# Channel-mixer weights split by two DMAs and ACT instead of a load, ACT and DVE

## The chip, the cores and the metric

The kernel runs on one core of a Trainium2 chip. Five engines work side by side, each through its own queue in order: PE (TensorE, matrix products), DVE (VectorE), ACT (ScalarE), POOL (GpSimd) and SP (SyncE, which here only issues transfers); 16 DMA engines move data between the chip's memory (HBM) and the on-chip memory (SBUF). The metric is the device time of one execution in microseconds. The trace of one execution is read beside the times.

## The reference, cut to what matters

One encoder layer on 512 tokens of width 1024, all in float32. An attention part (two token mixers, gates, output projection) gives `x`; then comes the channel mixer, which the change touches, and a last norm:

```python
h = rms_norm(x, norm_ffn[l])
x = x + (jax.nn.silu(h @ w_gate_ffn[l]) * (h @ w_up_ffn[l])) @ w_down_ffn[l]
return rms_norm(x, norm_final)
```

`w_gate_ffn` and `w_up_ffn` are 1024 x 2816, `w_down_ffn` is 2816 x 1024.

## The kernel before

PE multiplies fast in float32r, a rounded form of float32. To keep float32's accuracy every operand is split in two float32r tiles: `hi`, the rounded value, and `lo`, what rounding left (value minus `hi`). `mm3` (L87) then adds three products, hi x hi, hi x lo and lo x hi; lo x lo is left out.

Weights come in units of 128 x 1024 float32 (512 KB). `load_unit` (L77) does four things for one unit: SP issues a load into a raw tile (three buffers, tag `raw`), ACT rounds it into `whi` (`split_hi`, L68), and DVE subtracts `whi` from the raw tile into `wlo` (`split_lo`, L75). `whi` and `wlo` have five buffers each, used in turn by all units of the program. A buffer is free again when PE has done the unit's last product.

The channel mixer works with 66 units. The 2816 hidden features are 22 blocks of 128 (`f` = 0 to 21). For each, `gu(f)` loads a gate unit (`fg`) and an up unit (`fu`); `ffn_in` (L596) runs 8 x 3 products for each over the 512 tokens, applies a sigmoid on ACT and two multiplications on DVE, and splits the result into `ah` and `al`. The first two blocks are done in two token halves of 256. From `f` = 3 on, after every second block, `down0(u)` adds one unit of the output weights (`d0`, two hidden blocks by 512 output columns) for the four token tiles. After block 21 the second 512 output columns follow, with 11 more units (`d1`); the last two of them are loaded together and used token tile by token tile, so that each tile's last norm and output can start early. In the middle of the stage units are thus used in groups of five: gate, up, gate, up, down.

Ahead of the channel mixer stands the output projection (`w_out`, units `o0` and `o1`). Its second half holds four units until its last token tile is done; each token tile's norm (`norm_tile`, L531) uses ACT, DVE and a power on POOL (L108), and PE transposes the result.

The order on each engine is not written out: a scheduler of the framework sorts the instructions by a model of their times when the program is built, and sets the signals between the engines. Each engine then works through its list in order, and an instruction that waits for a signal holds up all behind it on its engine.

Of the kernel before, what the change touches and what calls it, by code (L numbers as in the profile page):

```python
# [9 lines left out]
F32 = mybir.dt.float32  # L10
F32R = mybir.dt.float32r
AF = mybir.ActivationFunctionType
ALU = mybir.AluOpType
# [6 lines left out]
P = 128  # L20
# [7 lines left out]
UNIT = 1024  # L28
# [6 lines left out]
def kernel(  # L35
# [19 lines left out]
    v, a, g, pe = nc.vector, nc.scalar, nc.gpsimd, nc.tensor  # L55

    def pool(stack, name, bufs=1, space=None, side=None):
        kw = {} if space is None else {"space": space}
        if side is not None:
            kw["side"] = side  # L60
        return stack.enter_context(tc.tile_pool(name=name, bufs=bufs, **kw))
# [3 lines left out]
    wp = pool(ctx, "wp", bufs=5)  # L65

    def split_hi(dst, src):
        a.copy(dst, src)  # L68
# [5 lines left out]
    def split_lo(dst, src, hi):  # L74
        v.tensor_tensor(out=dst, in0=src, in1=hi.bitcast(F32), op=ALU.subtract)  # L75

    def load_unit(src, nm, n=UNIT, raw_tile=None):  # L77
        raw = wp.tile([P, UNIT], F32, tag="raw", bufs=3, name=f"raw_{nm}") if raw_tile is None else raw_tile
        raw = raw[:, :n]
        nc.sync.dma_start(raw, src)  # L80
        hi = wp.tile([P, UNIT], F32R, tag="whi", name=f"whi_{nm}")[:, :n]
        lo = wp.tile([P, UNIT], F32R, tag="wlo", name=f"wlo_{nm}")[:, :n]
        split_hi(hi, raw)
        split_lo(lo, raw, hi)
        return hi, lo

    def mm3(acc, lh, ll, rh, rl, start, stop):  # L87
# [48 lines left out]
    for u in range(4):  # L136
        xr = up.tile([P, UNIT], F32, tag="u", name=f"xr{u}")
        if u < 2:
            rkv = up.tile([P, UNIT], F32, tag="u", name=f"rkv{u}")
        if u == 0:  # L140
            khi = wp.tile([P, UNIT], F32R, tag="whi", name="whi_akv0")
            klo = wp.tile([P, UNIT], F32R, tag="wlo", name="wlo_akv0")
            units_kv.append((khi, klo))
            for j in range(2):
                c = slice(j * S, (j + 1) * S)
                nc.sync.dma_start(xr[:, c], xT[0][:, c])
                nc.scalar.dma_start(rkv[:, c], w_in[4][:, c])
            for j in range(2):
                c = slice(j * S, (j + 1) * S)
                split_scaled(xgh[:, j, :], xgl[:, j, :], xr[:, c], gmix[:, j:j + 1])  # L150
                split_hi(khi[:, c], rkv[:, c])
                split_lo(klo[:, c], rkv[:, c], khi[:, c])
        else:
            nc.sync.dma_start(xr, xT[u])
            if u == 1:
                units_kv.append(load_unit(w_in[5], "akv1", raw_tile=rkv))
            for j in range(2):
                kt = 2 * u + j
                split_scaled(xgh[:, kt, :], xgl[:, kt, :], xr[:, j * S:(j + 1) * S], gmix[:, kt:kt + 1])
        xrs.append(xr)  # L160
    units_q = [load_unit(w_in[u], f"aq{u}", raw_tile=up.tile([P, UNIT], F32, tag="u", name=f"raq{u}")) for u in range(4)]
    for u in range(4):
        sq = up.tile([P, 2, S], F32, tag="u", name=f"sqx{u}")
# [156 lines left out]
    def group_b(h, parts):  # L320
        us = [load_unit(w_in[6 + 4 * h + u, :, :768], f"b{h}_{u}", 768) for u in range(4)]
        vt = u_tile(f"vb{h}", shape=(P, NT, 2, P))
        qT = u_tile(f"qTb{h}")
        kT = [u_tile(f"kTb{h}_{i}") for i in range(2)]
        for tt in range(NT):
            nm = f"b{h}_{tt}"
            t = slice(tt * P, (tt + 1) * P)
            acc = ps_mm.tile([P, S], F32, tag="mm", name=f"acc_{nm}")[:, :384]
            for kt in range(KT):
                hi, lo = us[kt // 2]  # L330
                o = (kt % 2) * 384
                mm3(acc, xgh[:, kt, t], xgl[:, kt, t], hi[:, o:o + 384], lo[:, o:o + 384], kt == 0, kt == KT - 1)
            z = tmp.tile([P, S], F32, tag="q", name=f"z_{nm}")
            a.activation(z[:, :128], acc[:, :128], AF.Copy, scale=rstd8[:, tt:tt + 1])
            a.activation(z[:, 128:384], acc[:, 128:384], AF.Copy, scale=rstd[:, tt:tt + 1])
            split_hi(vt[:, tt, 0, :], z[:, 256:384])
            split_lo(vt[:, tt, 1, :], z[:, 256:384], vt[:, tt, 0, :])
            qs = pack_heads(do_rope(z[:, :256].rearrange("p (n h d) -> p n h d", n=1, d=HD), tabs["b"], tt, nm), 4, 2, nm)
            transpose_heads([qs[:, 0, 0:P], qs[:, 1, 0:P]] + pair(qs, 2), [qT, kT[0]], tt, f"{nm}_0")
            transpose_heads(pair(qs, 3), [kT[1]], tt, f"{nm}_1")  # L340
            if tt == NT - 1:
                parts[:] = [qT, kT, vt]
            yield True
# [144 lines left out]
    for qd in range(4):  # L488
# [7 lines left out]
        for br in range(2):  # L496
            oh, ol = osplit[br]
            for j in range(2):
                ct = 2 * qd + j
                hi, lo = us[j]  # L500
# [110 lines left out]
    def down(acc, u, wu, tt, c0=0, c1=S):  # L611
        hi, lo = wu
        t = slice(tt * P, (tt + 1) * P)
        for j in range(2):
            f = 2 * u + j
            w = slice(j * S + c0, j * S + c1)
            mm3(acc, ah[:, f, t], al[:, f, t], hi[:, w], lo[:, w], f == 0, f == NF - 1)

    def gu(f):
        return load_unit(w_gu[2 * f], f"fg{f}"), load_unit(w_gu[2 * f + 1], f"fu{f}")  # L620

    acc0 = None

    def down0(u):
        wu = load_unit(w_down[u], f"d0_{u}")
        for tt in range(NT):
            down(acc0[tt], u, wu, tt)

    gu01 = [gu(0), gu(1)]
    for t0 in (0, 256):  # L630
        for f in range(2):
            ffn_in(f, t0, t0 + 256, *gu01[f])
    for f in range(1, NF):
        if f > 1:
            ffn_in(f, 0, S, *gu(f))
        if f == 1:
            acc0 = [ps_d.tile([P, S], F32, tag="pd", name=f"pd0_{tt}") for tt in range(NT)]
        if f >= 3 and f % 2 == 1:
            u = (f - 3) // 2
            down0(u)  # L640
    down0(10)

    s3 = const.tile([P, 3, NT], F32, name="s3")
# [18 lines left out]
                 (ps_g.tile([P, S], F32, tag="pg", name="pd1_4")[:, :H], H, S)])  # L662
    NLAST = 2
    for u in range(11 - NLAST):
        wu = load_unit(w_down[11 + u], f"d1_{u}")
        for tt in range(NT):
            for acc, c0, c1 in acc1[tt]:
                down(acc, u, wu, tt, c0, c1)
    last = [load_unit(w_down[11 + u], f"d1_{u}") for u in range(11 - NLAST, 11)]
    for tt in range(NT):  # L670
        for i, (acc, c0, c1) in enumerate(acc1[tt]):
            for u in range(NLAST):
# [96 lines left out]
```

## Time and profile before

| | us |
|---|---|
| median of 3 runs | 769.11 |
| lowest, highest | 768.08, 769.47 |
| the profiled execution | 766.71 |
| its span in the trace | 764.7 |
| PE, DVE, ACT, POOL busy in the span | 745.6, 412.5, 337.2, 102.7 |

Times in the trace are microseconds from the start of the span. A row of an instruction names its line in the kernel, its engine, what it writes and reads; names lose their numbers, so `wlo_fg` stands for all gate units. PE's matmuls overlap: the trace gives one some 0.39 us, but the next starts 0.23 us later, so PE's pace is read from starts. "Busy" of PE counts any time in which a matmul is under way. PEclk is the clock that PE was granted, as a share of 2.4 GHz. In the table of DMA issues the last number is the median time from issue to landing.

### The profile page before, as it was taken

How to read it: one execution, taken by the hardware profiler on the slowest of the kernel's cores; microseconds unless marked ns; L12 is line 12 of the kernel's file. 1: busy time of each engine (PE TensorE's matmuls, PEld its weight loads, DVE VectorE, ACT ScalarE, POOL GpSimd, SP SyncE). 2: the span in 40 equal slices, each digit the busy share in tenths (PEclk: the TensorE clock that was granted, in tenths of full speed). 3: DMA queues.
4: the chain of work that ended last, by engine and by line, in shares of the span. 5: the costliest groups of instructions: out<-in, count | busy, mean ns of one | idle time of the engine just before them, and what ended most of it. 6: DMA issues, size and time to landing. Idle time of an engine off the chain costs nothing.

```text
span 764.7 us, 9837 instructions
## 1 busy us (share of the span) xinstructions
PE 745.6 (97%) x3786; PEld 638.5 (83%) x3786; DVE 412.5 (54%) x668; ACT 337.2 (44%) x606; POOL 102.7 (13%) x126
## 2 busy tenths in 40 slices
PE   5999999999999999999999999999999999999996
PEld 4889887799988888888889888888888888888885
DVE  5778698669795564494375433332423333335114
ACT  6457698777667665232153222222222322233203
POOL 3656342223221010100000000000000000000001
PEclk9999999999999999999999999999999999999998
DMA  8122021002141212344223332323232333232202
GB/s 331 64 84 83 29 68 58 21 22 85 29 136 60 78 56 83 137 138 138 82 83 111 111 109 84 110 86 108 86 107 91 102 94 100 90 103 84 82 1 111
DMA packets 21071, 69.52 MB, mean 91 GB/s; under 512 B 2592, under 2 KB 2848, under 8 KB 21024
## 3 DMA queue, kind: packets, MB, share of 16 engines
q1 hardware_dynamic: 18432, 63.45, 25.1%
q10 hardware_dynamic: 2592, 5.45, 2.0%
q8 instruction: 30, 0.49, 0.3%
q14 instruction: 17, 0.14, 0.1%
HBM read 66.79 MB, written 2.10 MB: 90 GB/s over the span
## 4 chain that ended last, share of the span: by engine, by line
PE 94%; DVE 2%; DMA 2%; ACT 1%; issue 1%; POOL 0%; POOLq 0%; ACTq 0%; SPq 0%; DVEq 0%
PE pg L89 5%; PE pu L89 5%; PE pu L90 5%; PE pg L90 5%; PE pg L88 5%; PE pu L88 5%; PE pd L89 5%; PE pd L88 5%; PE pd L90 5%; PE gt L89 4%; PE gt L88 4%; PE gt L90 4%; PE acc_b L89 3%; PE acc_b L88 3%; PE acc_b L90 3%; PE pp L88 2%
## 5 line engine op out<-in xcount | busy, mean ns | idle before, releaser
L89 PE MATMUL pd<-wlo_d,ah 128*128 128x512 f32 (+1 forms) x198 | 72.5, 366 | 0.0
L88 PE MATMUL pd<-whi_d,ah 128*128 128x512 f32 (+1 forms) x198 | 72.4, 366 | 0.0
L90 PE MATMUL pd<-whi_d,al 128*128 128x512 f32 (+1 forms) x198 | 72.0, 365 | 0.0
L88 PE MATMUL pg<-hh,whi_fg 128*128 128x512 f32 (+1 forms) x192 | 71.4, 372 | 0.0
L90 PE MATMUL pu<-hh,wlo_fu 128*128 128x512 f32 (+1 forms) x192 | 71.4, 372 | 0.0
L89 PE MATMUL pg<-hl,whi_fg 128*128 128x512 f32 (+1 forms) x192 | 71.3, 371 | 0.0
L88 PE MATMUL pu<-hh,whi_fu 128*128 128x512 f32 (+1 forms) x192 | 71.3, 371 | 0.0
L89 PE MATMUL pu<-hl,whi_fu 128*128 128x512 f32 (+1 forms) x192 | 71.3, 371 | 0.0
L90 PE MATMUL pg<-hh,wlo_fg 128*128 128x512 f32 (+1 forms) x192 | 71.3, 371 | 0.0
L75 DVE TENSOR_TENSOR wlo_d<-raw_d,whi_d 128x1024 fp32r<-128x1024 f32 x22 | 26.9, 1225 | 72.4 <-ACT whi_d L68 72.4
L75 DVE TENSOR_TENSOR wlo_fg<-raw_fg,whi_fg 128x1024 fp32r<-128x1024 f32 x22 | 27.0, 1225 | 70.0 <-ACT whi_fg L68 69.9
L68 ACT CAST whi_d<-raw_d 128x1024 fp32r<-128x1024 f32 x22 | 23.2, 1053 | 85.4 <-issue 42.3
L68 ACT CAST whi_fg<-raw_fg 128x1024 fp32r<-128x1024 f32 x22 | 23.2, 1053 | 78.8 <-PE pg L89 41.2
L68 ACT CAST whi_fu<-raw_fu 128x1024 fp32r<-128x1024 f32 x22 | 23.2, 1053 | 72.7 <-PE pu L89 69.1
L88 PE MATMUL gt<-xgh,whi_g 128*128 128x512 f32 x128 | 50.6, 395 | 0.0
L90 PE MATMUL gt<-xgh,wlo_g 128*128 128x512 f32 x128 | 50.5, 395 | 0.0
L89 PE MATMUL gt<-xgl,whi_g 128*128 128x512 f32 x128 | 50.5, 394 | 0.0
L683 POOL TENSOR_TENSOR r<-mf,mhalf 128x1 f32<-128x1 f32 x4 | 2.3, 586 | 356.9 <-DVE mf L681 356.9
L607 DVE TENSOR_TENSOR sg<-pu,sg 128x512 f32<-128x512 f32 (+1 forms) x24 | 15.4, 646 | 54.8 <-PE pu L90 54.8
L89 PE MATMUL acc_b<-wlo_b,xgh 128*128 128x384 f32 x128 | 43.6, 341 | 0.0
L90 PE MATMUL acc_b<-whi_b,xgl 128*128 128x384 f32 x128 | 43.4, 339 | 0.0
L88 PE MATMUL acc_b<-whi_b,xgh 128*128 128x384 f32 x128 | 43.3, 339 | 0.0
(278 smaller groups left out, 1832.9 us busy)
## 6 DMA issues: line engine op xcount, KB each, us to landing
raw_fg<-in_w_gu_dram SPq DMA_DIRECT2D x22, 512.0 KB, 3.3
raw_fu<-in_w_gu_dram SPq DMA_DIRECT2D x22, 512.0 KB, 3.3
raw_d<-in_w_down_dram SPq DMA_DIRECT2D x22, 512.0 KB, 3.3
raw_g<-in_w_in_dram SPq DMA_DIRECT2D x16, 512.0 KB, 3.3
raw_b<-in_w_in_dram SPq DMA_DIRECT2D x16, 384.0 KB, 3.6
raw_p<-in_w_proj_dram SPq DMA_DIRECT2D x8, 512.0 KB, 3.3
raw_o<-in_w_out_dram SPq DMA_DIRECT2D x8, 512.0 KB, 3.3
raq<-in_w_in_dram SPq DMA_DIRECT2D x4, 512.0 KB, 7.3
```

The source lines that it names most:

```text
L68: a.copy(dst, src)
L75: v.tensor_tensor(out=dst, in0=src, in1=hi.bitcast(F32), op=ALU.subtract)
L88: pe.matmul(acc, lhsT=lh, rhs=rh, start=start, stop=False)
L89: pe.matmul(acc, lhsT=lh, rhs=rl, start=False, stop=False)
L90: pe.matmul(acc, lhsT=ll, rhs=rh, start=False, stop=stop)
L607: v.tensor_tensor(out=t_, in0=pu, in1=t_, op=ALU.mult)
L683: g.tensor_tensor(out=r3, in0=ms, in1=mhalf[:, 0:1], op=ALU.pow)
```

## The change

The channel mixer's 66 units no longer go through `load_unit` but through a new function, `load_unit_dma`. POOL issues a DMA that reads the float32 weights from HBM and writes them rounded, as float32r, into `whi`. ACT writes the negative of `whi` into `wlo`. POOL issues a second DMA that reads the same weights again and adds them to `wlo` where they land, so that `wlo` holds weight minus `whi`. Raw tiles and the subtraction on DVE are not used for these units. All other units stay with `load_unit`. The new function stands ahead of `mm3`, so later lines move down by eight in the changed kernel's own rows.

```diff
@@ -82,6 +82,14 @@
         lo = wp.tile([P, UNIT], F32R, tag="wlo", name=f"wlo_{nm}")[:, :n]
         split_hi(hi, raw)
         split_lo(lo, raw, hi)
+        return hi, lo
+
+    def load_unit_dma(src, nm):
+        hi = wp.tile([P, UNIT], F32R, tag="whi", name=f"whi_{nm}")
+        lo = wp.tile([P, UNIT], F32R, tag="wlo", name=f"wlo_{nm}")
+        g.dma_start(hi, src)
+        a.activation(lo, hi.bitcast(F32), AF.Copy, scale=-1.0)
+        g.dma_start(lo, src, accum_op=ALU.add)
         return hi, lo
...
     def gu(f):
-        return load_unit(w_gu[2 * f], f"fg{f}"), load_unit(w_gu[2 * f + 1], f"fu{f}")
+        return load_unit_dma(w_gu[2 * f], f"fg{f}"), load_unit_dma(w_gu[2 * f + 1], f"fu{f}")
...
     def down0(u):
-        wu = load_unit(w_down[u], f"d0_{u}")
+        wu = load_unit_dma(w_down[u], f"d0_{u}")
...
     for u in range(11 - NLAST):
-        wu = load_unit(w_down[11 + u], f"d1_{u}")
+        wu = load_unit_dma(w_down[11 + u], f"d1_{u}")
...
-    last = [load_unit(w_down[11 + u], f"d1_{u}") for u in range(11 - NLAST, 11)]
+    last = [load_unit_dma(w_down[11 + u], f"d1_{u}") for u in range(11 - NLAST, 11)]
```

The scheduler's lists change with it. In the middle of the channel mixer, SP's list before held the loads of one group of five units and the next, one row a unit (the name's first number is the block, the last is the tile's own):

```order
L80 DMA raw_fg8_5001<-in_w_gu_dram 128x1024
L80 DMA raw_fu8_5007<-in_w_gu_dram 128x1024
L80 DMA raw_fg9_5069<-in_w_gu_dram 128x1024
L80 DMA raw_fu9_5075<-in_w_gu_dram 128x1024
L80 DMA raw_d0_3_5137<-in_w_down_dram 128x1024
L80 DMA raw_fg10_5167<-in_w_gu_dram 128x1024
L80 DMA raw_fu10_5173<-in_w_gu_dram 128x1024
```

The same units now stand in POOL's list, two rows a unit (L90 the rounding DMA, L92 the adding one):

```order
L90 DMA whi_fg8_4982<-in_w_gu_dram 128x1024
L90 DMA whi_fu8_4987<-in_w_gu_dram 128x1024
L92 DMA wlo_fg8_4983<-in_w_gu_dram 128x1024
L92 DMA wlo_fu8_4988<-in_w_gu_dram 128x1024
L90 DMA whi_fg9_5048<-in_w_gu_dram 128x1024
L92 DMA wlo_fg9_5049<-in_w_gu_dram 128x1024
L90 DMA whi_fu9_5053<-in_w_gu_dram 128x1024
L90 DMA whi_d0_3_5114<-in_w_down_dram 128x1024
L92 DMA wlo_fu9_5054<-in_w_gu_dram 128x1024
L92 DMA wlo_d0_3_5115<-in_w_down_dram 128x1024
L90 DMA whi_fg10_5143<-in_w_gu_dram 128x1024
L90 DMA whi_fu10_5148<-in_w_gu_dram 128x1024
```

Between the rounding row and the adding row of a unit stands at most one other unit's rounding row, and the next pair begins behind the adding rows of the last.

At the start of the channel mixer POOL's list before held only the powers of the norm tiles (`r2`) and, after the whole stage, of the last norm (`r3`):

```order
L108 TENSOR_TENSOR rsb_3_3393<-ms_3394,mhalf_73 128x4
L108 TENSOR_TENSOR r2_0_4094<-ms_4095,mhalf_73 128x1
L108 TENSOR_TENSOR r2_1_4142<-ms_4143,mhalf_73 128x1
L108 TENSOR_TENSOR r2_2_4190<-ms_4191,mhalf_73 128x1
L108 TENSOR_TENSOR r2_3_4213<-ms_4214,mhalf_73 128x1
L683 TENSOR_TENSOR r3_0_6577<-mf_0_6573,mhalf_73 128x1
```

Now the DMAs of the first five units stand among them:

```order
L90 DMA whi_fu0_4256<-in_w_gu_dram 128x1024
L116 TENSOR_TENSOR r2_2_4190<-ms_4191,mhalf_73 128x1
L90 DMA whi_fg1_4261<-in_w_gu_dram 128x1024
L90 DMA whi_fu1_4266<-in_w_gu_dram 128x1024
L90 DMA whi_fg2_4499<-in_w_gu_dram 128x1024
L92 DMA wlo_fu0_4257<-in_w_gu_dram 128x1024
L116 TENSOR_TENSOR r2_3_4213<-ms_4214,mhalf_73 128x1
L92 DMA wlo_fg1_4262<-in_w_gu_dram 128x1024
L92 DMA wlo_fu1_4267<-in_w_gu_dram 128x1024
L92 DMA wlo_fg2_4500<-in_w_gu_dram 128x1024
```

The power of the third norm tile stands behind one rounding DMA, that of the fourth behind four of them and the first of their adding DMAs.

## Rows read from the trace of the kernel before

**Rows 1.** Head of the page: span; busy time of each engine.
```profile
span 764.7 us, 9837 instructions
...
PE 745.6 (97%) x3786; PEld 638.5 (83%) x3786; DVE 412.5 (54%) x668; ACT 337.2 (44%) x606; POOL 102.7 (13%) x126
```

**Rows 2.** Table by stretches, two stretches of the channel mixer.
```profile
core 0: us, PE busy (x) PEld busy (x) DVE busy (x) ACT busy (x) POOL busy (x), PEclk, DMA share, GB/s
...
585.00:640.00 55.00, 55.00 (x245) 45.53 (x244) 20.42 (x23) 14.59 (x18) 0.00 (x0) 1.00 0.30 96
...
695.00:750.00 55.00, 55.00 (x294) 47.58 (x293) 13.22 (x19) 9.95 (x15) 0.00 (x0) 1.00 0.14 48
```

**Rows 3.** Timeline of PE, end of the output projection (start, duration).
```profile
389.75 0.48 PE L88 MATMUL po<-whi_o,yh 128*128 128x512 f32 x1
...
393.93 0.39 PE L88 MATMUL po<-whi_o,yh 128*128 128x512 f32 x1
...
395.29 0.28 PE L88 MATMUL pg<-hh,whi_fg 128*128 128x256 f32 x1
395.40 0.28 PE L89 MATMUL pg<-hl,whi_fg 128*128 128x256 f32 x1
```

**Rows 4.** Timeline of SP's queue, one group of five loads.
```profile
460.46 0.33 SPq L80 DMA_DIRECT2D raw_d<-in_w_down_dram  x1
465.94 0.33 SPq L80 DMA_DIRECT2D raw_fg<-in_w_gu_dram  x1
...
487.66 0.33 SPq L80 DMA_DIRECT2D raw_d<-in_w_down_dram  x1
```

**Rows 5.** Groups of instructions (count, busy us, mean ns, idle before, releaser).
```profile
L75 DVE TENSOR_TENSOR wlo_fg<-raw_fg,whi_fg 128x1024 fp32r<-128x1024 f32 x22 | 27.0, 1225 | 70.0 <-ACT whi_fg L68 69.9
...
L68 ACT CAST whi_fg<-raw_fg 128x1024 fp32r<-128x1024 f32 x22 | 23.2, 1053 | 78.8 <-PE pg L89 41.2 <-issue 31.6 <-PE po L90 4.4
...
L377 POOL TENSOR_SCALAR p_a<-p_a,r_a 128x512 f32<-128x512 f32 x32 | 22.7, 711 | 53.1 <-DVE r_a L355 48.0 <-PE sc_a L348 1.9 <-PE ptp_a L361 1.2
```

**Rows 6.** Timelines of ACT and DVE, start and middle of the channel mixer.
```profile
394.17 1.06 ACT L68 CAST whi_fu<-raw_fu 128x1024 fp32r<-128x1024 f32 x1 [0.31 <-PE po L90]
...
395.81 1.22 DVE L75 TENSOR_TENSOR wlo_fu<-raw_fu,whi_fu 128x1024 fp32r<-128x1024 f32 x1
...
562.48 0.59 ACT L605 ACTIVATE sg<-pg 128x512 f32<-128x512 f32 x1
...
567.88 0.61 ACT L68 CAST ah<-sg 128x512 fp32r<-128x512 f32 x1
```

**Rows 7.** Table by stretches, start of the program.
```profile
14.00:16.00 2.00, 1.33 (x11) 1.12 (x10) 1.62 (x3) 2.00 (x4) 1.92 (x2) 1.00 1.03 400
16.00:20.00 4.00, 0.43 (x4) 0.23 (x2) 4.00 (x2) 0.31 (x1) 3.74 (x2) 0.99 1.03 413
20.00:30.00 10.00, 9.58 (x59) 9.05 (x59) 9.89 (x13) 6.50 (x11) 7.06 (x6) 0.83 0.12 47
```

**Rows 8.** DMA issues (count, KB each, us from issue to landing).
```profile
raw_fg<-in_w_gu_dram SPq DMA_DIRECT2D x22, 512.0 KB, 3.3
...
raq<-in_w_in_dram SPq DMA_DIRECT2D x4, 512.0 KB, 7.3
...
out_dram<-xg SPq DMA_DIRECT2D x4, 256.0 KB, 2.0
```

**Rows 9.** Timeline of POOL, first and last power of the last norm.
```profile
752.03 0.54 POOL L683 TENSOR_TENSOR r<-mf,mhalf 128x1 f32<-128x1 f32 x1 [350.70 <-DVE mf L681]
...
759.99 0.55 POOL L683 TENSOR_TENSOR r<-mf,mhalf 128x1 f32<-128x1 f32 x1 [1.52 <-DVE mf L681]
```

**Rows 10.** Table by stretches, end of the program.
```profile
758.60:760.00 1.40, 0.00 (x0) 0.00 (x0) 1.29 (x5) 1.04 (x3) 0.01 (x1) 1.00 0.00 0
760.00:762.00 2.00, 0.00 (x0) 0.00 (x0) 0.49 (x1) 0.72 (x1) 0.53 (x1) 0.65 0.73 278
762.00:764.70 2.70, 0.00 (x0) 0.00 (x0) 0.00 (x0) 0.00 (x0) 0.00 (x0) 0.50 0.48 186
```

## The prediction

> **What bounds the kernel now.** I read the page's busy line first: PE is busy 745.6 of 764.7 us, DVE 412.5, ACT 337.2 [rows 1]. That is an average over stages, so the table by stretches came next. In the channel mixer, from 420 to 750 us, PE is busy for the whole of each of six stretches of 55 us (two stand in the group) at a granted clock of 1.00, that is 2.4 GHz; DVE, which the change relieves, is busy about 20 of 55 us in five of them [rows 2]. The matmul rows give PE's step: six 512-column matmuls start between 393.93 and 395.29, 0.2267 us each [rows 3]. A unit of weights feeds 24 of them (8 of 512 columns, three products each; for the output weights 2 x 4 x 3), so PE eats a unit in 24 x 0.2267 = 5.44 us, and the group of five that recurs (gate, up, gate, up, down) in 27.2 us. SyncE's load rows agree: from one raw_d to the next 487.66 - 460.46 = 27.20 us [rows 4]. So nothing taken off DVE can shorten this stage; the question is whether units still arrive every 5.44 us.
>
> **What is removed.** 66 subtractions on DVE, of which I take one of 1.225 us as the measure [rows 5]: 66 x 1.225 = 81 us of DVE. Their cover is PE's 5.44 us per unit, so they are worth 0. The 66 loads on SyncE go; they were issued when a subtraction freed a raw tile, three units ahead of need, and nothing waited for them. ACT loses 66 rounding copies of 1.053 us [rows 5] and gains 66 negations. No negation is in the trace; the nearest rows on ACT are these copies and the sigmoid of 512 columns at 0.59 beside a copy of 512 at 0.61 [rows 6], so I take 1.05, which changes nothing for ACT.
>
> **What is added.** 132 DMAs on POOL, until now idle in this stage, two for each unit, with a round trip between them: the rounded part must land, ACT must negate it, and only then may the adding DMA be issued. POOL's queue is worked in order, and the order listed in the section on the change settles the matter: the next unit's rounded load mostly stands behind the previous unit's adding DMA. With such a queue the five buffers no longer overlap the units freely. A group of five units holds three serial round trips: (fg8, fu8 together), (fg9), (fu9, d0_3 together).
>
> The parts of a round trip, bounded from rows:
> - h, the transfer of a rounded load. In the stage the DMA engines are busy 0.30 of the time with one load per 5.44 us: 1.63 us [rows 2]. In the crowded stretch from 14 to 16 us they moved 400 GB/s, which makes 524,288 bytes 1.31 us [rows 7]. I take 1.6. Whether rounding slows the transfer no row shows; the upper bound is twice, 3.2.
> - a, the transfer of an adding DMA. It reads the weights again, reads its destination in SBUF, and writes. Lower bound 1.3 as above, if the second read is free; upper bound 4.8, if two reads and a write each cost a whole transfer. The nearest row for an SBUF read by DMA is the output store, 256 KB in 2.0 us from issue to landing, beside 3.3 for a load of 512 KB [rows 8]: a read of SBUF costs about what a load of as many bytes does. So I take load plus read, 2 x 1.6 = 3.2.
> - r, the rest of a landing: 3.3 from issue to landing [rows 8], less SyncE's issue of 0.33 [rows 4], less 1.3: 1.7.
> - n, the negation and its signals: 1.05 + 0.05.
> - p, POOL's issue of one DMA. The lower bound is SyncE's 0.33 [rows 4]. POOL's own work takes 0.54 for one element per partition [rows 9] and 0.71 for 512 [rows 5]; two such pieces of work (a list of reads, one of writes) would be 1.4, the upper bound. I take 1.0.
>
> That one queue's transfers follow each other is seen at the start of the program, where four loads issued together land 7.3 us after issue, not 3.3 [rows 8]. So a round trip is p + (its adding transfers) + h + r + n: the hi transfer waits behind the adding ones issued before it. In a group the three trips carry all five adding transfers: 5a + 3(p + h + r + n) = 5a + 3 x 5.4 = 5a + 16.2. With a = 3.2 that is 32.2 us against PE's 27.2: 5.0 us late per group. The engines' own work is 5 x (1.6 + 3.2) = 24 us, under 27.2: what binds is the order in POOL's queue, not DMA capacity. It decides from a = (27.2 - 16.2)/5 = 2.2 on.
>
> In the second half of the down projection POOL does two trips for three units: 3 x 3.2 + 2 x 5.4 = 20.4 against 16.3, 4.1 late per three.
>
> At the start of the stage the mixer's first units used to lie in raw tiles, with 1.05 + 1.22 us on ACT and DVE to go [rows 6]. Now their loads wait until the output projection's last pass frees buffers: its last token tile begins at 389.75, and the first buffer is free six matmuls later, at about 391.3 [rows 3]. POOL issues four rounded loads before the first of their adding DMAs (the fourth waits for the pass's end, 395.3), so wlo_fu0 is issued at about 396.4 and lands p + a + r = 5.9 later, 402.3. PE has its 24 half matmuls of fg0 from 395.29 (2.9 us, 0.12 each [rows 3]), then parts that need only rounded weights and the last transposes: about 4 us are lost. POOL's power for the last norm tile stands behind wlo_fu0's DMA and moves by about as much, inside this loss.
>
> **The sum.** Some 44 units in 8.8 groups run at the late pace: 8.8 x 5.0 = 44. Twelve units of the output weights at the end, 4 x 4.1 = 16. Start 4. Less what is loaded ahead when the late pace begins, two units, 2 x 5.44 = 11. Together +53. The profiled execution took 766.71 us, so 820; the median of the runs shown, 769.11, lies 2.4 above it, so I say 822. Before any loss the end of the program is unchanged: POOL's last powers come after all its DMAs, as before [rows 9].
>
> Two prices stand only in the Trainium skill. Its page "Collectives: The Full Stack", section "The bandwidth ceiling: the fold count and why AG ≠ RS ≠ AR", says that an addition inside a DMA costs no cycles of its own but needs two reads, which halves the rate: by that a is twice a load, 3.2 with my 1.6 and 2.6 with 1.3, and the sum +53 or about +18. No run here shows it yet. The page "DMA: Bandwidth & Descriptors", section "Specifications", gives a first byte of about 1 us to DMAs issued from GpSimd and 0.6 to those from SyncE: 0.4 more per trip, +1.2 a group, and the sum +67.
>
> **Rivals.**
> - Hidden, not slower (or hardly). The place is the same queue, the price a. If an adding DMA is no dearer than a load, 1.3 to 1.6, a group takes 22.7 to 24.2 us, PE never waits in steady state, and the last twelve units need 15.6 per three, under 16.3. Only the start is left, 0 to 2 us: 767 to 771. For it: the read of SBUF may overlap the other read. Against it: every path of more than 2.2. Chance 0.22, half of it within the bound of 0.2% (1.5 us), which is about what a measurement of this kernel can tell from no change.
> - Dearer yet. If a = 4.8, a group is 40.2: 8.8 x 13.0 + 4 x 8.9 + 7 - 11 = +146, 915; if rounding doubles h as well as a = 3.2, three trips take 4.8 more: 53 + 42 + 13 = +108, 877. Chance 0.25.
> - The clock. PE idle from about 15 to 20 us was followed by a stretch at 0.83, and after its last matmul the granted clock fell from 1.00 to 0.5 (1.2 GHz) at about 760.6 [rows 7, 10]. With idle pieces of 1 to 4 us in each group PE might run partly at the lower level. A stretch of 10 us at 0.83 loses 1.7 us; three per group lose 5.1, about the slack of 5.0 that PE then has, so this is covered unless the clock stays down: PE at 1.2 GHz needs 54.4 a group, and the stage's 360 us would double, some 1,120. Chance 0.03 for most of that.
> - It doesn't do what it says: POOL's issue could be so cheap and landings so early that the start gains too, since the DVE is free for the first tiles. That is worth at most 1 to 3 us, 764 to 768. Chance 0.04.
>
> The forecast itself (a between 2.2 and 4, +10 to +100): 0.46. So faster by over 0.2% 0.05, within 0.2% 0.10, slower 0.85. The range runs from 769, the hidden case, to 930, the dear one with the later first byte; about 0.2 is outside, more of it above.
>
> **What would show it.** Right: PE idle in each group of the channel mixer, ended by the landing of wlo tiles or by ACT; one down unit to the next about 32 us apart where it was 27.2; ACT's negations waiting for the landing of whi tiles; POOL's DMAs waiting for ACT, seldom for PE; DVE some 81 us lighter. The hidden rival: PE full from 420 to 750 as now. The steps can be checked singly: the landing of the adding DMA against that of the rounded load, POOL's issue against 1.0, and the DMA engines' share, which should rise from 0.30 to about 24/32 = 0.75. I would be wrong in kind if PE waits for its weights although POOL's queue stands empty, or if the loss sits at the start alone.

## The result, and the profile after

The changed kernel takes 814.86 us (median of four runs, 814.28 to 816.40), the kernel before 768.60 (four runs, 767.55 to 769.47): ratio 1.0606, 95% interval 1.0593 to 1.0620. It is slower by 46 us; 822 was forecast. The profiled execution took 814.78 us, its span is 812.6.

From the page of the changed kernel: span, busy time of each engine, DMA queue of POOL (packets, MB, share of 16 engines), the chain that ended last, and the landings of a `fu` unit's two DMAs.

```profile
span 812.6 us, 9858 instructions
...
PE 763.2 (94%) x3786; PEld 647.0 (80%) x3786; DVE 338.1 (42%) x602; ACT 336.2 (41%) x606; POOL 196.2 (24%) x258
...
q0 software_dynamic: 19008, 69.21, 36.6%
...
PE 46%; issue 35%; POOL 10%; DMA 5%; DVE 2%; ACT 2%; POOLq 0%; SPq 0%; ACTq 0%; DVEq 0%
...
whi_fu<-in_w_gu_dram POOLq DMA_DIRECT2D x22, 512.0 KB, 6.6
wlo_fu<-in_w_gu_dram POOLq DMA_DIRECT2D x22, 512.0 KB, 5.6
```

DVE's busy time fell by 74 us [rows 1] and ACT kept its 336, yet the span grew by 47.9. The chain that ended last is PE for only 46% of the span; the rest runs through POOL, the transfers and "issue", time in which the engine waited for nothing that the profile shows. The table by stretches shows where PE stopped being full; the first of these rows answers to [rows 2].

```profile
585.00:640.00 55.00, 50.59 (x213) 40.76 (x213) 7.61 (x11) 13.33 (x17) 12.20 (x17) 0.97 0.73 173
640.00:695.00 55.00, 52.32 (x230) 42.55 (x229) 8.30 (x12) 13.83 (x18) 14.16 (x20) 1.00 0.75 175
```

PE is busy 50.6 of 55 us where it was 55.0, and does 213 matmuls (rows that the trace holds) where it did 245. The DMA share (second number from the right) rose from 0.30 to 0.73.

Four starts of PE's matmuls cut the stage into three parts: the first gate product, the first and the last down product, and the last up product between them. Timeline of PE before (the first gate product, 395.29, stands in [rows 3]):

```profile
441.83 0.39 PE L88 MATMUL pd<-whi_d,ah 128*128 128x512 f32 x1
...
686.40 0.39 PE L90 MATMUL pu<-hh,wlo_fu 128*128 128x512 f32 x1
...
758.30 0.28 PE L90 MATMUL pd<-whi_d,al 128*128 128x256 f32 x1
```

And after:

```profile
395.92 0.28 PE L96 MATMUL pg<-hh,whi_fg 128*128 128x256 f32 x1
...
448.97 0.39 PE L96 MATMUL pd<-whi_d,ah 128*128 128x512 f32 x1
...
720.17 0.39 PE L98 MATMUL pu<-hh,wlo_fu 128*128 128x512 f32 x1
...
805.96 0.28 PE L98 MATMUL pd<-whi_d,al 128*128 128x256 f32 x1
```

Start of the stage: 46.54 us before, 53.05 after, +6.5. Groups of five: 244.57 and 271.20, +26.6. Output weights at the end: 71.90 and 85.79, +13.9. Together +47.0; of the rest, 0.6 was there before the stage began and 0.2 lies behind its last product. The same cut is made for every kernel below, each time in its profiled execution, which lies up to 3.4 us off the median of that kernel's runs.

POOL's timeline, three round trips, shows what sets the pace (L90 issues a rounding DMA, L92 an adding one; in brackets the idle time before, and what ended it):

```profile
509.59 0.87 POOL L92 DMA_DIRECT2D wlo_fg<-in_w_gu_dram  x1 [7.26 <-ACT wlo_fg L91]
511.06 0.85 POOL L92 DMA_DIRECT2D wlo_fu<-in_w_gu_dram  x1 [0.60 <-ACT wlo_fu L91]
511.61 0.86 POOL L90 DMA_DIRECT2D whi_fg<-in_w_gu_dram  x1
520.21 0.85 POOL L92 DMA_DIRECT2D wlo_fg<-in_w_gu_dram  x1 [7.74 <-ACT wlo_fg L91]
520.75 0.88 POOL L90 DMA_DIRECT2D whi_fu<-in_w_gu_dram  x1
521.29 0.89 POOL L90 DMA_DIRECT2D whi_d<-in_w_down_dram  x1
528.42 0.87 POOL L92 DMA_DIRECT2D wlo_fu<-in_w_gu_dram  x1 [6.24 <-ACT wlo_fu L91]
529.64 0.86 POOL L92 DMA_DIRECT2D wlo_d<-in_w_down_dram  x1 [0.35 <-ACT wlo_d L91]
530.19 0.87 POOL L90 DMA_DIRECT2D whi_fg<-in_w_gu_dram  x1
530.73 0.88 POOL L90 DMA_DIRECT2D whi_fu<-in_w_gu_dram  x1
539.06 0.88 POOL L92 DMA_DIRECT2D wlo_fg<-in_w_gu_dram  x1 [7.45 <-ACT wlo_fg L91]
```

POOL issues a rounding DMA and stands for 6 to 8 us until ACT has negated what it brought. A trip with two adding DMAs takes 10.62 us (509.59 to 520.21, 528.42 to 539.06), one with a single adding DMA 8.21. The three make 29.5 us for five units (29.4 in the two groups that follow); PE needs 27.2 [rows 4]. The table of waits of the stage from 420 us on names the links (waits, times, longest):

```profile
ACT wlo_fg L91 <- DMA whi_fg<-in_w_gu_dram: 135.9, 19, 9.6
POOL wlo_fg L92 <- ACT wlo_fg L91: 134.2, 19, 9.7
...
POOL whi_fg L90 <- PE pu L98: 2.3, 1, 2.3
```

ACT waits for the landing, POOL for ACT, and POOL for PE once, 2.3 us: buffers are not what is short. In the DMA engines' busy tenths, 505 to 532 us in 40 slices of 0.675 us, the trips are seen as gaps:

```profile
DMA  9999980003999999999600003988999993000969
```

In each trip the engines work for about 7 us and then stand for 2 to 3, while the last transfer's landing is signalled, ACT negates and POOL issues.

At the start of the stage, the table by stretches; then the issue of a DMA by POOL and the row of PE that waits for it:

```profile
402.00:404.00 2.00, 0.00 (x0) 0.00 (x0) 0.72 (x2) 1.78 (x3) 0.88 (x2) 0.85 0.99 195
404.00:406.00 2.00, 0.37 (x1) 0.38 (x2) 1.40 (x3) 0.52 (x2) 0.41 (x1) 0.50 1.10 219
406.00:408.00 2.00, 2.00 (x11) 2.00 (x11) 0.00 (x0) 0.00 (x0) 0.00 (x0) 0.50 1.04 262
408.00:410.00 2.00, 2.00 (x11) 2.00 (x11) 0.00 (x0) 0.00 (x0) 0.00 (x0) 0.50 1.03 270
410.00:412.00 2.00, 2.00 (x18) 2.00 (x17) 0.85 (x2) 0.41 (x1) 0.00 (x0) 0.94 1.11 225
```

```profile
397.49 0.89 POOL L92 DMA_DIRECT2D wlo_fu<-in_w_gu_dram  x1 [0.59 <-ACT wlo_fu L91]
...
405.63 0.58 PE L98 MATMUL pu<-hh,wlo_fu 128*128 128x256 f32 x1 [3.98 <-DMA wlo_fu<-in_w_gu_dram]
```

PE stood 3.98 us for the adding DMA of wlo_fu0, and the granted clock (third number from the right) fell from 1.00 to 0.50, that is from 2.4 to 1.2 GHz, and stayed there until about 410.

### The profile page after: what moved, and what is told of

Its sections match the earlier page's. It is cut to its first block, busy times and chain, and to the rows that moved or that the text cites. A ratio compares the mean times of both kernels' runs of the same rounds, so it can differ in the third digit from the quotient of the medians.

```text
span 812.6 us, 9858 instructions
## 1 busy us (share of the span) xinstructions
PE 763.2 (94%) x3786; PEld 647.0 (80%) x3786; DVE 338.1 (42%) x602; ACT 336.2 (41%) x606; POOL 196.2 (24%) x258
## 3 DMA queue, kind: packets, MB, share of 16 engines
q1 hardware_dynamic: 8928, 28.84, 10.5%
## 4 chain that ended last, share of the span: by engine, by line
PE 46%; issue 35%; POOL 10%; DMA 5%; DVE 2%; ACT 2%; POOLq 0%; SPq 0%; ACTq 0%; DVEq 0%
PE gt L97 4%; PE gt L96 4%; PE gt L98 3%; PE acc_b L97 3%; PE acc_b L96 3%; PE acc_b L98 3%; DMA whi_d<-in_w_down_dram 2%; POOL whi_d L90 2%; PE pp L96 2%; PE pp L97 2%; PE po L98 2%; PE pp L98 2%; PE po L97 2%; PE po L96 2%; POOL wlo_fg L92 2%
## 5 line engine op out<-in xcount | busy, mean ns | idle before, releaser
L91 ACT ACTIVATE wlo_fg<-whi_fg 128x1024 fp32r<-128x1024 f32 x22 | 23.3, 1060 | 145.0 <-DMA whi_fg<-in_w_gu_dram 145.0
L75 DVE TENSOR_TENSOR al<-sg,ah 128x512 fp32r<-128x512 f32 (+1 forms) x24 | 15.6, 648 | 155.3 <-ACT ah L68 155.3
L614 DVE TENSOR_TENSOR sg<-pg,sg 128x512 f32<-128x512 f32 (+1 forms) x24 | 15.5, 647 | 111.3 <-ACT sg L613 111.3
L98 PEld LDWEIGHTS pu<-hh,wlo_fu 128*128 128x128 f32 x192 | 38.9, 202 | 27.3 <-DMA wlo_fu<-in_w_gu_dram 20.7
L91 ACT ACTIVATE wlo_d<-whi_d 128x1024 fp32r<-128x1024 f32 x22 | 23.3, 1060 | 75.3 <-DMA whi_d<-in_w_down_dram 75.1
L92 POOL DMA_DIRECT2D wlo_fg<-in_w_gu_dram x22 | 19.0, 863 | 140.3 <-ACT wlo_fg L91 140.3
L91 ACT ACTIVATE wlo_fu<-whi_fu 128x1024 fp32r<-128x1024 f32 x22 | 23.3, 1059 | 69.9 <-DMA whi_fu<-in_w_gu_dram 66.1
L96 PE MATMUL gt<-xgh,whi_g 128*128 128x512 f32 x128 | 50.6, 395 | 0.0
L97 PEld LDWEIGHTS pd<-wlo_d,ah 128*128 128x128 f32 x198 | 38.1, 192 | 11.9 <-DMA wlo_d<-in_w_down_dram 5.6
L96 PEld LDWEIGHTS pd<-whi_d,ah 128*128 128x128 f32 x198 | 38.2, 193 | 11.7 <-ACT ah L68 4.3
L98 PEld LDWEIGHTS pg<-hh,wlo_fg 128*128 128x128 f32 x192 | 36.2, 188 | 11.4 <-DMA wlo_fg<-in_w_gu_dram 5.2
```

Source lines behind the costliest of these rows:

```text
L91: a.activation(lo, hi.bitcast(F32), AF.Copy, scale=-1.0)
L92: g.dma_start(lo, src, accum_op=ALU.add)
L96: pe.matmul(acc, lhsT=lh, rhs=rh, start=start, stop=False)
L97: pe.matmul(acc, lhsT=lh, rhs=rl, start=False, stop=False)
L98: pe.matmul(acc, lhsT=ll, rhs=rh, start=False, stop=stop)
L614: v.tensor_tensor(out=t_, in0=pg, in1=t_, op=ALU.mult)
```

## The experiments

The theory: the loss is the order in POOL's queue, by which the next unit's rounding DMA stands behind an adding DMA that waits for ACT; and, apart from that, the longer chain of the first unit. The rivals: the DMA engines are short of capacity, POOL's issues are dear, or buffers are short. In each table or text below the three parts of the stage are meant as cut above; before they are 46.5, 244.6 and 71.9 us.

**1. Another order in POOL's queue.** Same DMAs, same ACT work; each adding DMA stands behind the rounding DMAs of the two units that follow (fixed by edges of order without a signal, from the sixth unit on). The cut of the code is condensed.

```
 def load_unit_dma(src, nm):
-    g.dma_start(hi, src)
-    a.activation(lo, hi.bitcast(F32), AF.Copy, scale=-1.0)
-    g.dma_start(lo, src, accum_op=ALU.add)
+    # per unit k: rounding DMA and negative of unit k + 2, then the adding DMA of unit k
+    while len(his) <= min(k + AHEAD, len(plan) - 1):   # AHEAD = 2
+        pinned(g.dma_start(hi, plan[j][0]), j)
+        a.activation(lo, hi.bitcast(F32), AF.Copy, scale=-1.0)
+        ...
+        pinned(g.dma_start(his[k][1], plan[k][0], accum_op=ALU.add), k)
```

> From the sixth unit on, POOL's list is pinned so that each adding DMA stands behind the rounding DMAs of the next two units; the same 132 DMAs, the same bytes, the same buffers. Queue theory (the changed kernel is late because each round trip of rounding DMA, ACT and adding DMA holds up the next unit's rounding DMA in POOL's queue): the trips overlap, a group of five is back at PE's 27.2 us, only the start of the stage stays lost (about 7 us): 772 to 778. Transfer theory (the DMA engines cannot carry the 132 transfers at PE's pace): still about 815, down units 29.4 us apart. Buffer theory (rounding DMAs wait for PE to free one of five buffers): 815 or more, POOL's idle time ended by PE.

Measured: 775.25 us, ratio 1.0088 (1.0072 to 1.0105). The parts are 52.8, 244.6 and 71.9: groups and end cost nothing any more, the start all of it. Its table by stretches and POOL's timeline:

```profile
585.00:640.00 55.00, 55.00 (x245) 45.53 (x244) 8.87 (x13) 15.25 (x19) 14.97 (x22) 1.00 0.90 194
```

```profile
530.50 0.55 POOL L112 DMA_DIRECT2D whi_fu<-in_w_gu_dram  x1 [4.00 <-PE pu L124]
531.03 0.91 POOL L100 DMA_DIRECT2D wlo_fu<-in_w_gu_dram  x1
536.17 0.55 POOL L112 DMA_DIRECT2D whi_d<-in_w_down_dram  x1 [4.23 <-PE pd L124]
536.70 0.91 POOL L100 DMA_DIRECT2D wlo_fg<-in_w_gu_dram  x1
```

PE is full at a clock of 1.00; the DMA engines carry all the adding transfers at a share of 0.90, and POOL now waits for PE to free a buffer. Order is shown as the cause for groups and end; capacity, POOL's issue and buffers fall as rivals.

**2. The second DMA without the addition.** The tile `lo` then holds the weights themselves, so this kernel leaves out the remainder.

```
-    g.dma_start(lo, src, accum_op=ALU.add)
+    g.dma_start(lo, src)
```

> The second DMA of each unit does not add: it is a second rounding load over ACT's negative (the remainder is left out). POOL's order and the waits are as in the changed kernel. Queue theory with the price of the adding transfer as the term that decides: a falls from the 2.4 us that the trips of the changed kernel show to about 1.6, a group takes 3 x 5.8 + 5 x 1.6 = 25.4, under 27.2; the last twelve units need 16.4 per three, about PE's 16.3; the start loses about 6: 772 to 778. If the trips cost the same whatever the second DMA does (latency alone, not its transfer): 805 to 815.

Measured: 771.91 us, 1.0047 (1.0032 to 1.0062), just under the range expected; parts 52.0, 244.6, 71.9. Without the addition the groups take what they took before. From the page:

```profile
q0 software_dynamic: 19008, 69.21, 27.7%
```

27.7% of 772.5 us over 132 DMAs is 1.62 us of the 16 engines for each. All of them round, the second ones too, since `lo` is a float32r tile as well; I had taken 1.6 for a load (experiment 7 has plain loads and rounding ones side by side). In the channel mixer POOL's and ACT's instructions stand in the same order as in the changed kernel, so here the price of the transfer alone makes the difference: without the addition the same serial trips fit under PE's 27.2 us. That is the forecast's hidden rival with its condition met by force.

**3. Rounding on ACT, adding DMA kept.** The raw load is SP's again, ACT rounds and negates, POOL issues adding DMAs alone.

```
-    g.dma_start(hi, src)
+    raw = wp.tile([P, UNIT], F32, tag="raw", bufs=3, name=f"raw_{nm}")
+    nc.sync.dma_start(raw, src)
+    split_hi(hi, raw)
```

> Only the remainder goes by DMA: SP loads a raw tile, ACT rounds it and then writes the negative, POOL issues the adding DMA. The DMA engines carry the same bytes (a plain load in place of the rounding one), ACT does one instruction of 1.05 us more per unit, POOL issues 66 DMAs that no longer have a round trip between them. Queue theory: groups at 27.2 us; the start still has one adding DMA in the way of each of the first units, up to 6 us: 768 to 776. Transfer theory: about 815. ACT theory (a second pass per unit on ACT delays the sigmoid): ACT has 27 of 55 us busy at most, no loss.

Measured: 772.86 us, 1.0059 (1.0037 to 1.0081); parts 51.8, 244.6, 71.9. The adding DMAs are all there, the DMA share is 0.83 from 530 to 585 us, and PE is full: the addition by itself costs nothing when nothing behind it in its queue is needed for the next. POOL's queue now holds only adding DMAs, so it gives their price:

```profile
q0 software_dynamic: 9504, 34.61, 25.7%
```

25.7% of 773.5 us over 66 is 3.01 us of the 16 engines. The Trainium skill ("Collectives: The Full Stack", section "The bandwidth ceiling: the fold count and why AG ≠ RS ≠ AR") says of collectives that two reads halve the rate; 3.01 against 1.62 is 1.86 times, near it.

**4. The first four units loaded as before.**

```
 def gu(f):
-    return load_unit_dma(w_gu[2 * f], f"fg{f}"), load_unit_dma(w_gu[2 * f + 1], f"fu{f}")
+    ld = load_unit if f < 2 else load_unit_dma
+    return ld(w_gu[2 * f], f"fg{f}"), ld(w_gu[2 * f + 1], f"fu{f}")
```

> The first four units are made as before (load, ACT, DVE), the other 62 by DMA. Queue theory: the start's loss (4 us of waiting and some 2 to 3 of PE at its lower clock after it) goes, the groups and the last units stay late: 805 to 810. If the loss sat at the start alone: about 768.

Measured: 803.89 us, 1.0452 (1.0427 to 1.0476), a little better than the 805 to 810 expected. The start is gone as a loss (46.5, clock 1.00 from 400 to 420 us), and the trips are as long as in the changed kernel (10.5, 8.35, 10.6 us from 530.80 on). The two other parts are also shorter than in the changed kernel, 265.3 and 82.4, in an execution that was the fastest of its four (800.45). Most of the groups' difference lies in the second group: 29.85 us from one down unit's first product to the next (471.68 to 501.53), where the changed kernel has 35.08 (476.17 to 511.25). That units loaded ahead of POOL's first trips give this lead is likely, but not shown.

**5. Both: the order of 1 and the start of 4** (the edit against 1).

```
-    AHEAD, OLD, PIN = 2, 0, 5
+    AHEAD, OLD, PIN = 2, 4, 5   # units below OLD by load_unit
```

> Both losses taken out together: POOL's DMAs are ordered as in e1_order_ahead2 and the first four units are loaded, rounded and subtracted as before. Theory (two separate losses, the order of POOL's queue and the first unit's longer chain, and nothing else): 1.0088 less what e4_old_start gave at the start, 11 us at most and 6 to 7 by PE's wait and low clock, so 766 to 770 us, within 0.3 % of before; no PE wait for wlo_fu0 and the granted clock at 1.00 from 400 to 420 us. Rival (the casting and adding transfers cost something all through, by DMA engines that are busy 0.9 of the time): 772 to 776 us with PE waits spread over the stage.

Measured: 768.80 us against 768.35, 1.0009 (1.0000 to 1.0018); parts 46.5, 244.6, 71.9, those of before to 0.01 us. Two rows of its table by stretches:

```profile
400.00:420.00 20.00, 20.00 (x170) 20.00 (x169) 7.27 (x15) 7.01 (x14) 3.75 (x6) 1.00 0.44 117
...
585.00:640.00 55.00, 55.00 (x244) 45.54 (x243) 8.31 (x12) 15.25 (x19) 14.98 (x22) 1.00 0.90 194
```

So the two losses are the whole of it. DVE is free of the subtractions in 62 of 66 units, and the kernel is no faster: they were worth nothing, as they lay beside a full PE.

**6. One unit ahead instead of two** (the edit against 1).

```
-    AHEAD, OLD, PIN = 2, 0, 5
+    AHEAD, OLD, PIN = 1, 0, 5
```

> As e1_order_ahead2, with each adding DMA behind the rounding DMA of one unit more instead of two. Theory (one round trip of POOL's queue then serves two units): a trip holds one rounding and one adding transfer, the landing, ACT's negative and the issues, 8.2 to 9.8 us by the trips of the changed kernel with one adding transfer, so 4.1 to 4.9 us a unit against PE's 5.44: the groups stay at 27.2 us, and the time is e1_order_ahead2's 775 us, 773 to 779. Rival (a unit's pitch is one whole trip at one unit ahead as well, since rounding DMAs wait for the buffer or for the adding one before): 8.2 us a unit for 54 units, over 900 us. Second rival (landings lengthen as the DMA engines fill, 6.6 to 7.2 us): 10.6 to 11.2 us for two units, 780 to 790 us.

Measured: 775.91 us, 1.0085 (1.0062 to 1.0107); parts 53.2, 244.6, 71.9. One round trip that serves two units is enough. POOL's timeline shows the smaller reserve, about 1 us of waiting for ACT, hidden by the wait for PE ahead of it:

```profile
565.61 0.55 POOL L112 DMA_DIRECT2D whi_d<-in_w_down_dram  x1 [4.04 <-PE pd L124]
567.06 0.87 POOL L100 DMA_DIRECT2D wlo_fu<-in_w_gu_dram  x1 [0.90 <-ACT wlo_fu L113]
570.83 0.55 POOL L112 DMA_DIRECT2D whi_fg<-in_w_gu_dram  x1 [2.90 <-PE pg L124]
```

**7. Rounding by DMA, remainder by DVE.** Two transfers a unit, on two queues, and no adding DMA that waits for ACT's negative.

```
+    raw = wp.tile([P, UNIT], F32, tag="raw", bufs=3, name=f"raw_{nm}")
+    nc.sync.dma_start(raw, src)
     g.dma_start(hi, src)
-    a.activation(lo, hi.bitcast(F32), AF.Copy, scale=-1.0)
-    g.dma_start(lo, src, accum_op=ALU.add)
+    split_lo(lo, raw, hi)
```

> Only the rounded part comes by a casting DMA on POOL's queue; the remainder is again DVE's, from a raw load on SP's queue. Same two transfers a unit, none of them adding, and no instruction of POOL waits for ACT. Theory (the loss is POOL waiting in order for ACT between two transfers): the groups are at PE's 27.2 us, PE's clock 1.00, and only the start may lose 0 to 4 us: 767 to 774 us. Rival (the casting DMA by itself, on POOL's queue, is what is late: POOL's arithmetic and waits delay it): PE waits for whi tiles in the groups, 780 us or more.

Measured: 770.99 us, 1.0033 (1.0021 to 1.0046). Its parts are 46.5, 244.6 and 71.9: nothing is lost in the stage, not even at its start. The profiled execution's span is 769.7 us, 5.0 above before: 2.6 of it lie ahead of the stage (first gate product at 397.93) and 2.4 behind its last product. What lies ahead arises in the first 30 us of the program, where the edit changes nothing: there the clock was 0.57 and 0.74 in two stretches in which the changed kernel had 0.66 and 1.00.

```profile
20.00:25.00 5.00, 3.22 (x15) 3.22 (x16) 4.96 (x8) 3.04 (x5) 4.78 (x6) 0.57 0.27 105
25.00:30.00 5.00, 5.00 (x27) 4.70 (x27) 5.00 (x5) 3.46 (x7) 2.54 (x2) 0.74 0.00 0
```

The profiled executions of experiments 2, 3, 4 and 6 also begin the stage late, at 397.67 to 398.26, so some 2 to 3 us of their spans do not belong to the stage. Why these builds differ there was not tried. The five runs of experiment 7 agree (769.97 to 771.52), so its 2.6 us over the median of before are not the chance of one run.

Its two queues give the price of a rounded load beside a plain one:

```profile
q1 hardware_dynamic: 18432, 63.45, 24.0%
q0 software_dynamic: 9504, 34.61, 14.2%
```

POOL's 66 rounding DMAs take 14.2% of 769.7 us, 1.66 us of the 16 engines each; SP's plain loads take 24.0% for 63.45 MB, 1.53 us per 512 KB. Rounding adds little.

**8 and 9. The negative made twice; and the order laid down, nothing else.** In both, POOL's DMAs follow each other in the changed kernel's own order, fixed by edges; 9 is the control. The cut of the code shows the negative alone.

```
-    a.activation(lo, hi.bitcast(F32), AF.Copy, scale=-1.0)
+    for _ in range(NEG):   # 2 in the one, 1 in the control
+        a.activation(lo, hi.bitcast(F32), AF.Copy, scale=-1.0)
```

> The changed kernel, with ACT's negative made twice into the same tile (the second gives what the first gave), POOL's DMAs pinned in the changed kernel's own order. Each unit's chain is 1.06 us longer; no transfer, no POOL instruction and nothing of PE is added, and ACT is busy some 19 of 55 us instead of 13. Theory A (POOL's round trips are serial, three for five units, and inside a trip the adding transfers follow each other on the DMA engines, 3.0 us each): one 1.06 a trip, 3.2 us a group, 8.8 groups and 8 trips at the end: 815 + 28 + 8 = 851, 845 to 858; trips of 11.7 and 9.3 us where they were 10.6 and 8.2. Theory B (a trip with two units is 2.4 us longer because the second adding DMA is issued after the second negative, not because of its transfer): two 1.06 in such a trip, 5.3 us a group: 815 + 47 + 13 = 875, 865 to 885; trips of 12.7 and 9.3. Rival (what binds is the DMA engines' or POOL's own work, the chain is hidden): 814 to 820.

> The same pinning with one negative, so nothing but the way in which the order is laid down differs from the changed kernel: 813 to 817 us. If it is far from that, e8_two_negations is to be read against this run and not against the changed kernel.

Measured: 851.95 us (1.1093, 1.1048 to 1.1137) and 809.05 (1.0534, 1.0510 to 1.0559). The control missed its 813 to 817. Its instructions stand in the same order on every engine in the stage; its parts are 51.5, 265.6 and 87.2. At the start PE waited 2.80 us for wlo_fu0 where it had waited 3.98, and the clock stayed at 1.00; that part is shorter by 1.6 us of the 5.8. The rest, 5.6 us in the groups less 1.4 at the end, stays open: from 494 to 611 us its trips are 10.3 to 10.5 and 8.1 to 8.5 us, hardly shorter, but the changed kernel has single trips that are longer (one landing of 9.2 us at 599.86), and a clock of 0.97 in stretches where the control has 1.00.

Against the control, the second negative costs 42.9 us; theory A gave 36, theory B 60. The total agrees with A less well than it looks: the parts are 55.5, 303.2 and 88.9, so the groups lost 37.6 (A: 28, B: 47) and the end 1.7 (A: 8, B: 13). PE's list differs from the control's in 48 of its 3786 places, too. The trips say more. From about 500 to 630 us, those with one adding DMA went from 8.23 to 9.58 us (means of four each), those with two from 10.50 to 11.97 (nine and eight); over the whole of the groups' part the medians went from 8.5 to 9.5 and from 10.4 to 11.8. So a trip of one grew by 1.0 to 1.35 and a trip of two by 1.35 to 1.5, where B asks for 1.06 and 2.1: the second unit's negative is not a second whole link, and this is nearer to A, in which the transfers inside a trip follow each other on the DMA engines. That a trip of two grew by more than A's 1.06 was not explained. POOL's timeline of this kernel, a trip of one and a trip of two:

```profile
534.70 0.85 POOL L123 DMA_DIRECT2D wlo_fg<-in_w_gu_dram  x1 [8.54 <-ACT wlo_fg L120]
544.75 0.87 POOL L123 DMA_DIRECT2D wlo_fu<-in_w_gu_dram  x1 [8.08 <-ACT wlo_fu L120]
547.27 0.86 POOL L123 DMA_DIRECT2D wlo_d<-in_w_down_dram  x1 [1.64 <-ACT wlo_d L120]
557.29 0.89 POOL L123 DMA_DIRECT2D wlo_fg<-in_w_gu_dram  x1 [8.04 <-ACT wlo_fg L120]
```

The rival (the chain is hidden, no change) falls a second time.

## Why the prediction was right, and which terms were off

- **What bounds, and what the removal is worth.** PE full at 1.00, DVE's subtractions worth 0: right. Experiment 5 has almost none of them, experiment 7 all of them, and in both the stage is as long as before.
- **The mechanism.** One queue in order, three serial trips for five units: right, shown by experiments 1 (another order), 6 (one trip for two units) and 8 (a longer link). The trips, not the transfers' sum of 24 us per group, bind, and the price of the adding transfer decides whether they do (experiment 2); the DMA share was forecast at 0.75 and is 0.73 in the stretch shown.
- **The size of a trip** was the main term that was off: 11.8 and 8.6 us forecast, 10.6 and 8.2 measured, so a group of 29.4 instead of 32.2. The parts: a 3.2 forecast, 3.0 by experiment 3; h 1.6, and 1.6 by experiment 2; n 1.06 in the trace; r, 1.7, was not measured by itself. What remains is p, 1.0 in each trip: the rounding DMAs start 0.54 apart (520.75, 521.29), the adding one took up to 0.9, and these issues lie beside transfers that are still under way. Without p the trip of two is 1.7 + 2 x 3.0 + 1.6 + 1.1 = 10.4 (10.6 measured); the trip of one is 7.4, and 8.2 measured, with two rounded loads started together.
- **The lead** of two units (11 us) did not last: PE's first down units start 27.20 apart, the next 35.08 (448.97, 476.17, 511.25). By the usual trips a group is 2.2 us late and 8.8 of them are 19, but the groups' part lost 26.6; with -11 it would have been 8. Some trips and one group (588.51 to 620.48, 32.0 us) were longer than the usual, for reasons not looked into. These errors have opposite signs: 44 - 11 = 33 was forecast for this part, so the sum came out well in part by the luck of their cancelling.
- **The end:** 16 forecast, 13.9 measured; three units take 18.9 us (751.55 to 770.40), not 20.4, for the same reason as the trips.
- **The start:** 4 forecast. PE's wait is 3.98, ended by wlo_fu0 as said, but that number is luck: wlo_fu0 was there at 405.6 and not at 402.3, since from its issue at 397.49 it took 8.1 us instead of 5.9, behind four rounded loads; and PE had work until 401.65, about 3.3 us longer than the forecast's own numbers imply. The part lost 6.5, as the clock fell during the wait and stayed at 1.2 GHz for some 4.5 us of work, about 2.3 us by half the pace (an estimate from these rows); the prediction had considered the clock for the groups only. The control, with a wait of 2.80 and no fall, lost 4.9.
- **The clock rival** was right to be small in the groups: 0.94 to 1.00 in the stretches of 55 us.
- **The sum:** +53 forecast, +47 measured in the stage. DVE became 74 us lighter, not 81, which plays no part in it. The side sum of "about +18" for a load of 1.3 and an adding DMA of 2.6 does not come out of its terms: it is +20 with h left at 1.6 and +10 with h at 1.3 too. The forecast does not use it.

## What to carry to other kernels

Where a DMA queue is worked in order, a DMA that waits for another engine holds up every transfer behind it: issue the loads of the next units ahead of it; here one unit was enough. A price per transfer that is below the consumer's pace says nothing until one has counted how many round trips stand one after the other. And work taken off an engine that lies beside a full one is worth nothing, so such a change can only be paid for by what it puts in its place.

## What the runs showed of the hardware that I had not expected

- A rounding DMA from POOL costs little more than a plain load: 1.62 us of the 16 engines for 512 KB (experiment 2), 1.66 against 1.53 side by side (experiment 7); the adding one costs 3.01 (experiment 3).
- POOL's issue of a rounding DMA took 0.53 to 0.55 us (experiments 1, 2 and 7; in the changed kernel's crowded pairs the rows read 0.86 and overlap), of an adding one 0.85 to 0.91; SP's took 0.33 [rows 4].
- PE's wait of 3.98 us took the clock to 1.2 GHz, and it stayed there for some 4.5 us after PE had resumed (405.63 to about 410); in the control a wait of 2.80 us at the same place left it at 1.00.
- The DMA engines kept PE's pace at a busy share of 0.90 (experiments 1 and 5), with landings of 5.4 us for the rounded and 7.8 for the adding DMAs.
